# Another rule for the place of split weights, and the state space constants on VectorE alone, woven over a longer stretch

## The chip, the cores and the metric

The kernel runs on one core of a Trainium2 chip. The metric is the device time of one execution in microseconds (us), as the median of several runs. Engines are named as the profile names them: PE is TensorE's matmul, PEld its weight load, DVE is VectorE, ACT is ScalarE, POOL is GpSimd, SP is SyncE, whose queue only issues transfers here.

## What is computed

Two blocks follow each other on 512 tokens (528 with 16 meta tokens in the first) of width 1024. All is float32.

```python
# first block, two layers l = 0, 1
h = h + 0.5 * swiglu(rms_norm(h), ffn1_w_gu[l], ffn1_w_down[l])      # D_FF = 2816
u = rms_norm(h); c_q, c_kv, k_pe, hq, hf, hi, hg, ga, gb = split_cols(u @ w_in[l])
y_a = mla(c_q, c_kv, k_pe, ...) @ w_proj_attn[l]                     # 8 attention heads
y_b = hgrn2(hq, hf, hi, hg, ...) @ w_proj_rec[l]                     # 4 recurrent heads
merged = sigmoid(ga) * y_a + sigmoid(gb) * y_b
h = h + merged @ w_out[l]
h = h + 0.5 * swiglu(rms_norm(h), ffn2_w_gu[l], ffn2_w_down[l])
# second block: an S5 state space branch and a sparse attention branch, merged alike, then a fifth FFN
s = associative_scan(a, b)     # a, b from A_re, A_im, log_dt, B_re, B_im
y = C_re s_r - C_im s_i + D_skip u
```

The state space branch is computed in chunks of eight steps. For that it needs tables worked out from its parameters alone: powers of the complex decay times the input, output and feedback matrices. These are the constants of this case. They depend on nothing that the first block computes.

## The kernel before

Each float32 product is made of three matmuls on rounded operands: high by high, high by low and low by high. A weight is therefore loaded as a raw chunk of 512 KB (tile `raw`, four buffers, issued on SP's queue) and split into a high part `whi` (a copy on ACT) and a low part `wlo` (a subtraction on DVE, in plain stages on POOL for most chunks). Chunks are numbered by first use. There are H = 5 places for split chunks, each a pair of tiles.

**Places.** Chunk i goes into place i % 5, so it may be split only once chunk i - 5 was read for the last time (`allowed`, `hi_lo`). The splits are a queue of steps in order of first use. `between(cost)` is called as PE's work is emitted; it gives credit for steps, up to three at a time, and makes those that are allowed. A step that has not been made by then is made just before the chunk's first use.

**FFN.** There are five. The 22 column blocks j of the hidden layer come as six plain ones and sixteen made of seven products of twelve matmuls each (`product`, 1.46 us of PE in the program's own table of costs). The down projection is done in thirds; for the first two, its steps (`down_steps`, 0.73 us each, of six matmuls) are woven with the products of the next third. A down chunk (consumer operands `gh`, `gl`) is held for seven or eight such steps, with products between, while a chunk for products is read at once. In these stages every engine keeps the order in which the program emits (`self.pin`). The product's results leave the banks through ACT (`tu`, `zu`, `s`) and DVE (`c1`, `c2`, printed `c` in the profile); `gh` and `gl` follow.

**Mixer and merge.** The mixer weaves four pairs of attention and recurrent heads, j = 0 to 3, each with the dense work of the next. With j = 3, the last heads, the gates `ga` and `gb` are woven. Then `merge` follows: an item that frees tiles, eight `project` items (two projections, times gates, sum, split into `mgh` and `mgl`) and seven `w_out` items. Here the tile scheduler decides each engine's order.

**Constants.** `s5_setup_items` gives two lists of items, one for each layer of the first block. They are woven into the merge, from its second item to the fourth from the end. A complex product (`cmul`) is a DVE product `cm`, a POOL product `ct` and their sum, on POOL (tile `cm`) or on DVE (tiles `e`, or `cm` where the sign is turned). `within` makes the feedback matrices `ks` and stores them in 16 small pieces per item, 64 in all, into the DRAM tensor `s5_t` through SP's queue.

Of the kernel before, what the change touches and what calls it, by code (L numbers as in the profile page):

```python
# [281 lines left out]
class Kernel:  # L282
# [46 lines left out]
    def run(self):  # L329
# [6 lines left out]
        raws, sums, made = {}, {}, {}  # L336
        done = [False] * len(order)
        gone = [False] * len(loads)
        n_dma = used = 0
        credit = 0.0  # L340

        def load():
# [7 lines left out]
        def drop(c):  # L350
            raws.pop(c)
            gone[load_at[c]] = True
            while n_dma < len(loads) and (n_dma < self.RAW or gone[n_dma - self.RAW]):
                load()

        def hi_lo(i):
            if i not in made:
                made[i] = [self.wp.tile([128, 1024], F32R, tag=f"{x}{i % self.H}", name=f"w{x}_{i}") for x in ("hi", "lo")]
                n = 1024 if not isinstance(order[i], str) else CHUNKS[order[i]][1] * CHUNKS[order[i]][2]
                nk = 8 if not isinstance(order[i], str) else CHUNKS[order[i]][1]  # L360
                self.split_of[order[i]] = [t[:, :n].rearrange("p (k m) -> p k m", k=nk) for t in made[i]]
            return made[i]
# [62 lines left out]
        def allowed():  # L425
            if n_step == len(queue):
                return False
            i = queue[n_step][0]
            return i < self.H or done[i - self.H]

        def step():
            nonlocal n_step
# [13 lines left out]
                fn()  # L446

        self.between = between
        self.read = lambda c: done.__setitem__(index[c], True)
        load()  # L450
        self.setup(load)
        self.warm()
# [2 lines left out]
        for it in self.prog:  # L455
            if not (it.seven and self.pin):
                for i in range(used):
                    done[i] = True
            self.pin = it.seven
            if not it.seven:  # L460
                between(0.0)
                if it.chunks:
                    while allowed():
                        step()
            used += len(it.chunks)
            while n_step < len(queue) and queue[n_step][0] < used:
                assert allowed()
                step()
            it.fn()
# [540 lines left out]
    def mixer(self, l, st, nxt):  # L1010
# [136 lines left out]
        def hg_dense(j):  # L1147
            items = []
            for n, w in (("f", L), ("i", L), ("q", nq), ("g", nq)):
                items += dense(f"h{n}{l}.{j}", w, times_r(f"z{n}.{j}"))  # L1150
            return items
# [3 lines left out]
        def hg_start(j):  # L1155
            X = XS[j]
            zq, zf, zg = S.pop(f"zq.{j}"), S.pop(f"zf.{j}"), S.pop(f"zg.{j}")
            t = self.alloc("t")
            self.sc.activation(t[:, :L], zf[:, :L], AF.Sigmoid)
            k = self.alloc("k")  # L1160
            self.sc.activation(k[:, :L], zf[:, :L], AF.Sigmoid, scale=-1.0)
            t2 = self.alloc("t2")
            self.sc.activation(t2[:, :nq], zq[:, :nq], AF.Sigmoid)
            t3 = self.alloc("t3")
            self.sc.activation(t3[:, :nq], zg[:, :nq], AF.Sigmoid)
            if l > 0:
                nc.vector.tensor_scalar(t[:, :L], t[:, :L], self.olb[:, j:j + 1], self.lb1[:, j:j + 1], op0=OP.mult, op1=OP.add)
                nc.vector.tensor_scalar(k[:, :L], k[:, :L], self.olb[:, j:j + 1], None, op0=OP.mult)
            nc.vector.tensor_scalar(t[:, :L], t[:, :L], F_MIN, None, op0=OP.max)
            self.sc.preload_act_table_set("natural_log")  # L1170
            self.sc.activation(t[:, :L], t[:, :L], AF.Ln)
            nc.vector.tensor_tensor_scan(zf[:, :L], self.reset[:, :L], t[:, :L], 0.0, op0=OP.mult, op1=OP.add)
            nc.vector.scalar_tensor_tensor(zq[:, :nq], zq[:, :nq], 128 ** -0.5, t2[:, :nq], op0=OP.mult, op1=OP.mult)
            nc.gpsimd.tensor_tensor(zg[:, :nq], zg[:, :nq], t3[:, :nq], op=OP.mult)
            self.free(t, t2, t3)
            X.update(q=zq, b=zf, g=zg, k=k)
# [188 lines left out]
        self.prog += d0[h2:] + [Item(0.5, lambda: hg_start(0))] + qk_items(0)  # L1365
        gates = self.gate_items(str(l), nq, S, st)
        for j in range(4):
            nextd = hg_dense(j + 1) + [Item(0.5, lambda j=j: hg_start(j + 1))] + qk_items(j + 1) if j < 3 else gates
            if j == 2:
                def drop():  # L1370
                    for n in ("cq", "ckv"):
                        hs, ls = S.pop(n)
                        self.free(*hs, *ls)
                    self.free(S.pop("kr"))
                nextd = nextd + [Item(0.0, drop)]
            if j == 3:
                cut = len(gates) - len(gates) // 4
                self.prog += weave(att_items(j) + [Item(0.0, lambda: self.free(*S.pop("v")))], hg_items(j), gates[:cut])
                self.prog += [Item(0.0, lambda: (self.split_y(S, "ya", "ot", nq), self.split_y(S, "yb", "y", nq)))] + gates[cut:]
            else:  # L1380
                self.prog += weave(att_items(j), hg_items(j), nextd)

        at = len(self.prog)
        self.merge(str(l), nq, S, st, nxt)
        if l == 0:
            self.s5_items = self.s5_setup_items()
        m = self.prog[at:]
        self.prog[at:] = m[:1] + weave(m[1:-3], self.s5_items[l]) + m[-3:]


    def reduce_angle(self, t, w):
# [15 lines left out]
    def s5_setup_items(self):  # L1407
# [11 lines left out]
            while stores:  # L1419
                stores.pop(0)()  # L1420

        def store(*pairs, free=()):
            stores.append(lambda: ([nc.sync.dma_start(o, i) for o, i in pairs], self.free(*free)))
        mul, sub, add = OP.mult, OP.subtract, OP.add

        def tt(o, a, b, op, e=None):
            (e or nc.vector).tensor_tensor(o, a, b, op=op)

        def params():
            self.half_pi = self.cst.tile([128, 1], F32, name="half_pi")  # L1430
# [129 lines left out]
        def cmul(qr, s0, y, ri, apart=None):  # L1560

            sl = slice(4 * qr, 4 * qr + 4)

            def v(t):
                if apart is None:
                    return t[:, :512].rearrange("p (i q s) -> p i s q", i=4, s=8)
                return t[:, :512].rearrange("p (i s q) -> p i s q", i=4, s=8)
            pr, pi = (X[k][:, sl, s0:s0 + 8, None].to_broadcast([128, 4, 8, 16]) for k in ("pr", "pi"))  # L1570
            yr, yi = (y[:, 256 * i:256 * i + 256].rearrange("p (i q) -> p i q", q=16)[:, sl, None, :].to_broadcast([128, 4, 8, 16])
                      for i in range(2))
            o, t = self.alloc("cm"), self.alloc("ct")
            tt(v(o), pr, yi if ri else yr, mul)
            tt(v(t), pi, yr if ri else yi, mul, nc.gpsimd)
            if apart is not None:
                for g in range(2):
                    row = slice(64 * g, 64 * g + 64)
                    to = apart[g][32 * ri:32 * ri + 64, :512]
                    nc.vector.scalar_tensor_tensor(to, o[row, :512], -1.0 if ri else 1.0, t[row, :512], op0=mul, op1=sub)  # L1580
            elif ri == 2:
                nc.vector.scalar_tensor_tensor(o[:, :512], o[:, :512], -1.0, t[:, :512], op0=mul, op1=sub)
            else:
                tt(o[:, :512], o[:, :512], t[:, :512], add if ri else sub, nc.gpsimd)
            self.free(t)
            return o

# [21 lines left out]
        def within(qr):  # L1609
            e = X.pop("e")  # L1610
            ks = [self.alloc("ks"), self.alloc("ks")]
            ps = [self.bank(), self.bank()]
            for i in range(4):
                for g in range(2):
                    ti = 4 * qr + i
                    nc.tensor.matmul(ps[g][:16, 128 * i:128 * i + 128], X["cg"][g][:, 16 * ti:16 * ti + 16], e[g][:, 128 * i:128 * i + 128],
                                     start=True, stop=True)
            dd = X["dd"][:16, :32].rearrange("q (i g) -> q i g", g=2)[:, 4 * qr:4 * qr + 4]
            for g in range(2):
                kv = ks[g][:16, :512].rearrange("q (i s p) -> q i s p", i=4, s=8)  # L1620
                nc.vector.tensor_copy(ks[g][:16, :512], ps[g][:16, :512])
                w = self.small.tile([16, 4, 16], F32, name="dsk", bufs=2)
                tt(w, self.ident[:16, None, :16].to_broadcast([16, 4, 16]), dd[:, :, g:g + 1].to_broadcast([16, 4, 16]), mul)
                tt(kv[:, :, 0, :], kv[:, :, 0, :], w, add)
                dst = dr["t"].rearrange("(i g) q j c -> q g i j c", g=2)[:, g, 4 * qr:4 * qr + 4]
                store(*((dst[:, :, j, 16 * j:], ks[g][:16, :512].rearrange("q (i c) -> q i c", i=4)[:, :, :128 - 16 * j])
                        for j in range(8)), free=(ks[g],))
            self.free(*e)

        def in_done():  # L1630
# [468 lines left out]
```

## Time and profile before

| | |
|---|---|
| median of three runs | 3188.55 us (3185.94 to 3188.72) |
| the profiled execution's own time | 3189.57 us |
| its span, first to last instruction | 3187.5 us |
| mean granted clock of TensorE | 0.990 of full speed |
| DVE, ACT and POOL busy | 2182.0, 1436.9 and 785.6 us |

Busy times of engines overlap. The few per cent in which PE was not busy are what an order of work can change, besides the time lost at a lower granted clock. A wait in the profile is idle time before an instruction, put down to the engine and tile that released it last.

### The profile page before, as it was taken

The page shows a single profiled execution, that of the slowest core. Times are in us where ns is not written, and L with a number is a line of the kernel's source. Part 1 is how long each engine was busy: PE and PEld are TensorE (multiplying, and loading weights), DVE is VectorE, ACT ScalarE, POOL GpSimd, SP SyncE. Part 2 cuts the span into 40 slices and gives each one's busy share as a digit, 9 for nine tenths or more (in the row PEclk, how much of TensorE's full clock was granted, in tenths as well). Part 3 has the DMA queues.
Part 4 walks back from the last instruction along what each step waited for, and adds up shares of the span by engine and source line. Part 5 has one row for each costly group of instructions (what it writes and reads, how often), then busy time and mean ns, then how long its engine had stood idle before and what let it go on. Part 6 is the DMA issues. An engine that isn't in the chain of part 4 may idle for free. (4 is left out here: it accounts for less than half of the span.)

```text
span 3187.5 us, 52524 instructions
## 1 busy us (share of the span) xinstructions
PE 3100.3 (97%) x21338; PEld 2849.5 (89%) x21338; DVE 2182.0 (68%) x3752; ACT 1436.9 (45%) x2504; POOL 785.6 (25%) x461
## 2 busy tenths in 40 slices
PE   9999999999999999999999999899999989999999
PEld 9999998999999999999998888688988777788888
DVE  8666666756776666856666764977667587577674
ACT  5444444545444444434444544244446435444442
POOL 2000254444420002100034544530003553320001
PEclk9999999999999999999999999999999999999999
DMA  4232321112322223223321113332334432222332
GB/s 154 91 98 89 112 80 47 41 60 90 123 69 98 91 95 114 80 93 96 104 94 60 47 53 107 104 100 73 105 106 151 125 106 67 67 91 75 99 107 87
DMA packets 107682, 290.90 MB, mean 91 GB/s; under 512 B 23216, under 2 KB 33456, under 8 KB 107440
## 3 DMA queue, kind: packets, MB, share of 16 engines
q1 hardware_dynamic: 107440, 287.55, 28.0%
q8 instruction: 167, 2.74, 0.4%
q14 instruction: 75, 0.61, 0.1%
HBM read 273.61 MB, written 13.89 MB: 90 GB/s over the span
## 5 line engine op out<-in xcount | busy, mean ns | idle before, releaser
L249 POOL TENSOR_TENSOR wlo<-raw,whi 128x1024 fp32r<-128x1024 f32 (+1 forms) x185 | 470.0, 2543 | 2056.9 <-PE bank L249 1101.2
L249 ACT ACTIVATE whi<-raw 128x512 fp32r<-128x512 f32 (+2 forms) x664 | 541.5, 833 | 635.6 <-PE bank L249 301.5
L249 PE MATMUL bank<-xl,whi 128*128 128x264 f32 (+1 forms) x1992 | 664.1, 334 | 4.6 <-DVE xl L249 4.4
L249 PE MATMUL bank<-xh,whi 128*128 128x264 f32 (+1 forms) x1992 | 663.7, 334 | 0.7 <-ACT xh L249 0.7
L249 PE MATMUL bank<-xh,wlo 128*128 128x264 f32 (+1 forms) x1992 | 657.4, 330 | 1.3 <-POOL wlo L249 1.3
L249 DVE TENSOR_TENSOR wlo<-raw,whi 128x1024 fp32r<-128x1024 f32 (+2 forms) x399 | 410.0, 1030 | 156.4 <-ACT whi L249 153.2
L249 PE MATMUL bank<-gh,wlo 128*128 128x264 f32 (+1 forms) x1408 | 441.2, 313 | 15.3 <-DVE wlo L249 15.3
L249 PE MATMUL bank<-gh,whi 128*128 128x264 f32 (+1 forms) x1408 | 440.0, 312 | 0.0
L249 PE MATMUL bank<-gl,whi 128*128 128x264 f32 (+1 forms) x1408 | 439.9, 312 | 0.0
L249 PEld LDWEIGHTS bank<-xl,whi 128*128 128x128 f32 x1992 | 378.5, 190 | 34.1 <-DVE xl L249 6.3
L249 PEld LDWEIGHTS bank<-xh,whi 128*128 128x128 f32 x1992 | 378.1, 190 | 30.0 <-issue 4.1
L249 PEld LDWEIGHTS bank<-xh,wlo 128*128 128x128 f32 x1992 | 378.3, 190 | 27.2 <-issue 1.7
L249 PEld LDWEIGHTS bank<-gh,wlo 128*128 128x128 f32 x1408 | 265.6, 189 | 33.9 <-DVE wlo L249 18.4
L249 PEld LDWEIGHTS bank<-gl,whi 128*128 128x128 f32 x1408 | 265.4, 189 | 8.2
L249 PEld LDWEIGHTS bank<-gh,whi 128*128 128x128 f32 x1408 | 265.6, 189 | 7.8
L249 PE MATMUL bank<-T2h,whi 128*128 128x264 f32 (+1 forms) x640 | 183.8, 287 | 7.7 <-DVE c L249 6.3
L249 PE MATMUL bank<-T2h,wlo 128*128 128x264 f32 (+1 forms) x640 | 182.4, 285 | 2.2 <-DVE wlo L249 2.2
L249 PE MATMUL bank<-B21h,whi 128*128 128x264 f32 (+1 forms) x640 | 181.7, 284 | 1.0 <-ACT zu L249 0.9
L249 PE MATMUL bank<-B21l,whi 128*128 128x264 f32 (+1 forms) x640 | 181.6, 284 | 0.0
L249 PE MATMUL bank<-B21h,wlo 128*128 128x264 f32 (+1 forms) x640 | 181.4, 283 | 0.0
L249 PE MATMUL bank<-T2l,whi 128*128 128x264 f32 (+1 forms) x640 | 181.4, 283 | 0.0
L249 PE MATMUL bank<-T1l,whi 128*128 128x264 f32 (+1 forms) x640 | 181.1, 283 | 0.0
(373 smaller groups left out, 7054.1 us busy)
## 6 DMA issues: line engine op xcount, KB each, us to landing
raw<-in_w_dram SPq DMA_DIRECT2D x423, 512.0 KB, 3.5
raw<-in_w_dram SPq DMA_DIRECT2D x80, 448.0 KB, 3.2
h<-in_x_dram SPq DMA_DIRECT2D x8, 264.0 KB, 6.3
s_win<-cm SPq DMA_DIRECT2D x8, 256.0 KB, 2.9
s_t<-zero SPq DMA_DIRECT2D x8, 256.0 KB, 3.7
s_wo<-cm SPq DMA_DIRECT2D x16, 128.0 KB, 2.6
s<-s_win SPq DMA_DIRECT2D x8, 256.0 KB, 4.0
s<-s_wo SPq DMA_DIRECT2D x8, 256.0 KB, 4.9
```

The lines of the kernel that those rows point to most:

```text
L249: i = f(*args, **kw)
```

## The change

Three things are edited. The place of a split chunk is no longer i % 5: any place that was never used or whose chunk was read can be taken, and of those the one read longest ago is. The constants are woven from the start of the last heads (`at` is now taken at the start of each j, and so holds that of j = 3) up to all but the last two items of the merge. And `cmul` does both of its products and the sum on DVE, while the 64 small stores of `ks` are issued on ACT's queue.

```diff
+        places, read_at = [None] * self.H, list(range(-self.H, 0))
+        clock = 0
...
+        def vacant(k):
+            return places[k] is None or done[places[k]]
+
+        def read(i):
+            nonlocal clock
+            if not done[i]:
+                clock += 1
+                done[i] = True
+                for k in range(self.H):
+                    if places[k] == i:
+                        read_at[k] = clock
...
-                made[i] = [self.wp.tile([128, 1024], F32R, tag=f"{x}{i % self.H}", name=f"w{x}_{i}") for x in ("hi", "lo")]
+                at = min((k for k in range(self.H) if vacant(k)), key=lambda k: read_at[k])
+                places[at], read_at[at] = i, None
+                made[i] = [self.wp.tile([128, 1024], F32R, tag=f"{x}{at}", name=f"w{x}_{i}") for x in ("hi", "lo")]
...
-            i = queue[n_step][0]
-            return i < self.H or done[i - self.H]
+            return queue[n_step][0] in made or any(vacant(k) for k in range(self.H))
...
         for j in range(4):
+            at = len(self.prog)
...
-        at = len(self.prog)
         self.merge(str(l), nq, S, st, nxt)
...
-        self.prog[at:] = m[:1] + weave(m[1:-3], self.s5_items[l]) + m[-3:]
+        self.prog[at:] = weave(m[:-2], self.s5_items[l]) + m[-2:]
...
-            tt(v(t), pi, yr if ri else yi, mul, nc.gpsimd)
+            tt(v(t), pi, yr if ri else yi, mul)
...
-                tt(o[:, :512], o[:, :512], t[:, :512], add if ri else sub, nc.gpsimd)
+                tt(o[:, :512], o[:, :512], t[:, :512], add if ri else sub)
...
-                      for j in range(8)), free=(ks[g],))
+                      for j in range(8)), free=(ks[g],), queue=nc.scalar)
```

How instructions move: 24 `ct` and 12 `cm` instructions go from POOL to DVE, and 64 issues go from SP to ACT. PE has the same matmuls, in nearly the same order.

DVE in the first FFN, where the low part of down chunk 31 is made (`wlo_31`; chunks 30 and 32 are for products). Before:

```order
L249 TENSOR_TENSOR wlo_30_1661<-raw_22_1428,whi_30_1660 128x1024
L249 TENSOR_TENSOR raw_23_1592<-s1_187_1663,raw_22_1428 128x512
L249 TENSOR_TENSOR c2_178_1538<-bank_181_1541,zu_180_1540 128x264
L249 TENSOR_TENSOR c1_177_1537<-bank_186_1635,tu_179_1539 128x264
L249 SCALAR_TENSOR_TENSOR c2_178_1538<-c2_178_1538,s_189_1708 128x264
L249 SCALAR_TENSOR_TENSOR c2_178_1538<-bank_181_1541,s_189_1708 128x264
L249 TENSOR_TENSOR gl_191_1737<-c2_178_1538,gh_190_1736 128x528
L249 TENSOR_TENSOR wlo_31_1745<-raw_24_1649,whi_31_1744 128x1024
```

The same place now:

```order
L249 TENSOR_TENSOR wlo_30_1612<-raw_22_1428,whi_30_1611 128x1024
L249 TENSOR_TENSOR raw_23_1503<-s1_184_1614,raw_22_1428 128x512
L249 TENSOR_TENSOR wlo_31_1664<-raw_24_1600,whi_31_1663 128x1024
L249 TENSOR_TENSOR c2_179_1554<-bank_182_1557,zu_181_1556 128x264
L249 TENSOR_TENSOR s4_189_1714<-raw_23_1503,raw_22_1428 128x512
L249 TENSOR_TENSOR wlo_32_1712<-raw_23_1503,whi_32_1711 128x512
L249 TENSOR_TENSOR c1_178_1553<-bank_188_1650,tu_180_1555 128x264
```

The low part of chunk 31 stood behind the last five evacuations of a block j, and now stands ahead of three that follow.

DVE late in the merge of layer 1, around the sum of the gated projections of block 6 (`ga_6`, `gb_6`) and its split. Before:

```order
L249 TENSOR_TENSOR cm_2501_23176<-pr_2413_22565,s5b_2412_22563 128x4x8x16
L249 TENSOR_TENSOR dsk_23157<-ident_1072,s5d_2417_22573 16x64
L249 TENSOR_TENSOR ga_6_2405_22462<-bank_2471_22953,ga_6_2405_22462 128x512
L249 TENSOR_TENSOR gb_6_2407_22495<-bank_2472_22954,gb_6_2407_22495 128x512
L249 TENSOR_TENSOR ga_6_2405_22462<-ga_6_2405_22462,gb_6_2407_22495 128x512
L249 TENSOR_TENSOR cm_2517_23282<-pr_2413_22565,s5b_2412_22563 128x512
L249 TENSOR_TENSOR mgl_2474_22983<-ga_6_2405_22462,mgh_2473_22982 128x512
L249 TENSOR_TENSOR ga_7_2409_22528<-bank_2481_23023,ga_7_2409_22528 128x512
L249 SCALAR_TENSOR_TENSOR e_2503_23183<-cm_2517_23282,ct_2518_23283 64x512
L249 SCALAR_TENSOR_TENSOR e_2504_23184<-cm_2517_23282,ct_2518_23283 64x512
```

The same place now:

```order
L249 TENSOR_TENSOR ga_6_2440_22596<-bank_2487_23038,ga_6_2440_22596 128x512
L249 TENSOR_TENSOR gb_6_2444_22650<-bank_2488_23039,gb_6_2444_22650 128x512
L249 TENSOR_TENSOR wlo_411_22990<-raw_315_22780,whi_411_22989 128x1024
L249 TENSOR_TENSOR mgl_2486_23027<-ga_5_2411_22453,mgh_2485_23026 128x512
L249 TENSOR_TENSOR ga_6_2440_22596<-ga_6_2440_22596,gb_6_2444_22650 128x512
L249 TENSOR_TENSOR ga_7_2450_22693<-bank_2495_23087,ga_7_2450_22693 128x512
L249 TENSOR_TENSOR mgl_2490_23068<-ga_6_2440_22596,mgh_2489_23067 128x512
L249 TENSOR_TENSOR gb_7_2452_22726<-bank_2496_23088,gb_7_2452_22726 128x512
```

The constants between the merge's own instructions are gone here; they stand earlier, among the last heads and the first projections.

ACT among the last heads of layer 1, around the copy of weight chunk 397 (`p` is a softmax, `X` a decay, `pt` a transposed softmax). Before:

```order
L249 ACTIVATE whi_396_22044<-raw_300_21785 128x1024
L249 ACTIVATE X_2346_22082<-X_2346_22082 128x128x2 x2
L249 ACTIVATE whi_397_22103<-raw_301_21849 128x1024
L249 ACTIVATE p_2351_22118,sm_22120<-p_2351_22118,nm_22119 128x400
L249 ACTIVATE dq_2353_22134<-dk_2352_22133 128x512
```

The same place now:

```order
L249 ACTIVATE whi_396_22094<-raw_300_21812 128x1024
L249 ACTIVATE X_2367_22152<-X_2367_22152 128x128x2 x2
L249 DMA s5_t_74<-ks_2360_22106 16x4x128
L249 DMA s5_t_74<-ks_2360_22106 16x4x112
L249 DMA s5_t_74<-ks_2360_22106 16x4x96
L249 DMA s5_t_74<-ks_2360_22106 16x4x80
L249 ACTIVATE whi_397_22173<-raw_301_21886 128x1024
L249 DMA s5_t_74<-ks_2360_22106 16x4x64
L249 DMA s5_t_74<-ks_2360_22106 16x4x48
L249 DMA s5_t_74<-ks_2360_22106 16x4x32
L249 ACTIVATE p_2372_22188,sm_22190<-p_2372_22188,nm_22189 128x400
```

ACT now issues stores between its instructions, in four clusters of 16, of which this is the first.

## Rows read from the trace of the kernel before

**Rows 1.** The page's first part: busy us, share of the span, instructions.

```profile
PE 3100.3 (97%) x21338; PEld 2849.5 (89%) x21338; DVE 2182.0 (68%) x3752; ACT 1436.9 (45%) x2504; POOL 785.6 (25%) x461
```

**Rows 2.** PE's waits over the whole span: total us, times, longest us.

```profile
PE bank L249 <- DVE wlo L249: 17.5, 20, 1.8
...
PE bank L249 <- DVE c L249: 6.3, 8, 0.9
...
PE bank L249 <- ACT tu L249: 1.4, 3, 1.0
```

**Rows 3.** Timeline of 138 to 146 us: start, duration, engine, [idle before, releaser].

```profile
139.94 1.06 ACT L249 ACTIVATE whi<-raw 128x1024 fp32r<-128x1024 f32 x1 [2.46 <-PE bank L249]
...
141.28 0.28 PE L249 MATMUL bank<-gh,whi 128*128 128x264 f32 x1
...
141.40 0.28 PE L249 MATMUL bank<-gl,whi 128*128 128x264 f32 x1
...
142.19 1.22 DVE L249 TENSOR_TENSOR wlo<-raw,whi 128x1024 fp32r<-128x1024 f32 x1
...
143.47 0.39 PE L249 MATMUL bank<-gh,wlo 128*128 128x264 f32 x1 [1.78 <-DVE wlo L249]
```

**Rows 4.** Timeline of 218 to 228 us, DVE and PE.

```profile
225.62 1.22 DVE L249 TENSOR_TENSOR wlo<-raw,whi 128x1024 fp32r<-128x1024 f32 x1
...
227.84 0.39 PE L249 MATMUL bank<-T2h,whi 128*128 128x264 f32 x1 [0.89 <-DVE c L249]
```

**Rows 5.** Three windows: length, busy us of each engine, granted clock, DMA share, GB/s.

```profile
1008.60:1012.00 3.40, 3.40 (x16) 3.40 (x17) 3.40 (x7) 1.58 (x2) 0.00 (x0) 0.50 0.71 240
800.40:807.20 6.80, 6.04 (x27) 6.07 (x28) 6.80 (x11) 6.70 (x10) 3.16 (x2) 0.50 0.42 161
2056.50:2063.40 6.90, 4.18 (x10) 3.32 (x11) 6.81 (x8) 0.11 (x1) 2.11 (x2) 0.51 0.33 91
```

**Rows 6.** PE's waits in the merge of layer 0, 770 to 890 us.

```profile
PE bank L249 <- DVE ga L249: 5.1, 3, 3.0
PE bank L249 <- DVE gb L249: 1.9, 2, 1.7
```

**Rows 7.** PE's waits in the merge of layer 1, 2000 to 2110 us.

```profile
PE bank L249 <- DVE mgl L249: 3.7, 2, 3.0
PE bank L249 <- ACT mgh L249: 3.7, 1, 3.7
PE bank L249 <- DVE ga L249: 1.8, 1, 1.8
```

**Rows 8.** Windows: heads 0 to 2, last heads, merge; columns as in rows 5.

```profile
450.00:650.00 200.00, 194.96 (x1504) 180.43 (x1504) 138.07 (x344) 102.09 (x236) 96.37 (x79) 0.99 0.15 48
650.00:770.00 120.00, 120.00 (x962) 115.81 (x962) 64.74 (x170) 52.95 (x103) 49.67 (x30) 1.00 0.23 72
780.00:820.00 40.00, 33.01 (x241) 32.02 (x240) 39.15 (x49) 25.33 (x34) 27.87 (x14) 0.91 0.38 124
1690.00:1890.00 200.00, 188.10 (x1199) 166.64 (x1198) 133.31 (x291) 100.21 (x218) 98.73 (x76) 0.96 0.15 47
1890.00:2000.00 110.00, 110.00 (x558) 90.67 (x557) 58.31 (x104) 48.20 (x88) 52.81 (x33) 1.00 0.33 100
```

**Rows 9.** The constants' instructions by tile: ns least/median/most, first and last start.

```profile
L249 DVE TENSOR_TENSOR cm<-pr,s5b x16: 692/1186/2847, 1958.1 to 2061.2; 128x512 f32<-128x512 f32 x16
...
L249 POOL TENSOR_TENSOR cm<-cm,ct x12: 1263/1528/1992, 789.3 to 2053.1; 128x512 f32<-128x512 f32 x12
...
L249 POOL TENSOR_TENSOR ct<-pi,s5b x16: 1054/1501/1809, 1976.5 to 2065.4; 128x512 f32<-128x512 f32 x16
...
L1423 SPq DMA_DIRECT2D s_t<-ks x64: 325/424/1640, 2034.5 to 2096.3; - x64
```

**Rows 10.** Timeline of 794 to 800 us in the merge of layer 0, POOL and DVE.

```profile
795.72 2.83 POOL L249 TENSOR_TENSOR wlo<-raw,whi 128x1024 fp32r<-128x1024 f32 x1
...
796.23 2.89 DVE L249 TENSOR_TENSOR ga<-ga,gb 128x528 f32<-128x528 f32 x1
```

More of the change, by code (lines that the diff above doesn't have):

```diff
@@ L448, in run @@
         self.between = between
-        self.read = lambda c: done.__setitem__(index[c], True)
+        self.read = lambda c: read(index[c])
         load()
@@ L457, in run @@
                 for i in range(used):
-                    done[i] = True
+                    read(i)
             self.pin = it.seven
@@ L1420, in flush, with store, tt @@
                 stores.pop(0)()
-        def store(*pairs, free=()):
-            stores.append(lambda: ([nc.sync.dma_start(o, i) for o, i in pairs], self.free(*free)))
+        def store(*pairs, free=(), queue=nc.sync):
+            stores.append(lambda: ([queue.dma_start(o, i) for o, i in pairs], self.free(*free)))
         mul, sub, add = OP.mult, OP.subtract, OP.add
-        def tt(o, a, b, op, e=None):
-            (e or nc.vector).tensor_tensor(o, a, b, op=op)
+        def tt(o, a, b, op):
+            nc.vector.tensor_tensor(o, a, b, op=op)
         def params():
```

## The prediction

> **What bounds the kernel.** I read the busy shares first. PE is busy for 3100.3 of 3187.5 us [rows 1], so this kernel is PE's matmuls plus about 87 us of holes, plus what PE loses while its clock is lowered. DVE at 2182.0 us and POOL at 785.6 us have room on average. Nothing can be won here but holes and lowered clock; so the next view is the list of PE's waits, over the span and then by stretch.
>
> The largest entry of that list is the low part of a split weight, `wlo`: 17.5 us in 20 waits; `c`, an evacuation of the FFN's products, has 6.3 us in 8 [rows 2]. Taken FFN by FFN, the same list puts practically all of both into the five FFNs, four `wlo` waits in each. A timeline of one shows the mechanism [rows 3]. The copy `whi` of a down chunk starts on ACT at 139.94, after 2.46 us in which ACT waited for PE: its place was still held. From there on the chain is serial. ACT's copy ends at 141.00, DVE's subtraction runs from 142.19 to 143.41 behind another instruction, and PE, which had started `gl,whi` at 141.40, starts `gh,wlo` at 143.47. At this place PE's starts are 0.12 us apart (141.28, 141.40), so 1.95 us are lost where the profile shows an idle time of 1.78: 0.17 more per wait. The `c` waits have the same source. The late `wlo` of 1.22 us at 225.62 stands ahead of an evacuation on DVE, and PE waits 0.89 us for that at 227.84 [rows 4].
>
> The second cluster is the two merges. PE waits 5.1 + 1.9 = 7.0 us in that of layer 0 [rows 6] and 3.7 + 3.7 + 1.8 = 9.2 us in that of layer 1 [rows 7], for DVE's gated sums and their split. There DVE is full, 39.15 of 40 us, while among the last heads just before, it is busy for 64.74 of 120 us and 58.31 of 110, and PE there has no hole at all [rows 8].
>
> The third thing is the clock. Around such waits the granted clock falls to 0.50 of full speed, 1.2 instead of 2.4 GHz: for 3.40 us of PE's work right behind the `wlo` wait of the second FFN, for 6.04 us in the first merge and 4.18 us in the second, where PE had just stood for about 3 us [rows 5 to 7]. Work done at half speed loses half its time: 1.7, 3.0 and 2.1 us.
>
> **The places.** Before, a down chunk held for 7 or 8 woven steps keeps its place, and the chunk five later stands still though other places are vacant. With the new rule the queue of splits stops only when all five places are full. By the order of instructions `wlo_31` now stands ahead of the evacuations that it stood behind, and the low part of such a chunk is made 7 to 12 us of PE's work ahead of its use instead of 0 to 4. As 1.95 us was the longest delay, the waits should go: 17.5 + 6.3 us of idle time and 28 times 0.17 us are 28.6 us. What of it returns? At the ends of the thirds, products stand without down steps between, so PE asks for an evacuation every 1.46 us while the same splits have to be made. By the order I count up to 15 such places, three in each FFN, at which an evacuation may now be late. What such a lateness costs has no row for these places; the nearest is the wait for `tu`, 1.4 us in 3 [rows 2], or 0.47 us, and the mean of the `c` waits, 6.3 us in 8 or 0.79, is the upper end. I take 15 times 0.47 = 7.0 us; the bounds are 0 and 15 times 0.79 = 11.8. So the FFNs give 21.6 us (16.8 to 28.6), and the clock behind the `wlo` wait 1.7 more. Splitting as such costs nothing new: the same copies and subtractions run on the same engines.
>
> **The constants.** Three things happen to them. They start some 100 us earlier, from the beginning of the last heads. Their 24 `ct` and 12 `cm` go from POOL to DVE. And 64 stores go from SP to ACT.
>
> DVE gains 36 instructions. Their nearest rows are its own products `cm` of the same tile, 0.69 us at the least and 1.19 in the median [rows 9]: 36 of them are 24.8 to 42.8 us over both layers. Layer 1 has 20 of the 36, 13.8 to 23.8 us, and 16 `cm` that were already there, 19.0 us at the median; that is up to 42.8 us, and the last heads of layer 1 leave DVE 110 - 58.31 = 51.7 us free [rows 8]. In layer 0 the last heads leave 55.3 us. The cover of this term is therefore DVE's free time among the last heads, and if that cover failed the 24.8 to 42.8 us would come on top of merges that are already full. POOL loses 24 products and 12 sums at a median of 1.50 and 1.53 us [rows 9], about 54 us, which nothing waits for by itself.
>
> By the order, the late part of the merge of layer 1 loses its constants between `ga`, `gb` and `mgl`, but four or five groups of them remain among the first projections, as they do in smaller number in layer 0. I take all the waits of [rows 6, 7] as gone: 7.0 + 9.2 us, 9 waits at 0.17 us more, 1.5 us, and 3.0 + 2.1 us of clock, together 22.8 us. Its bounds are in the next term, as what remains and what comes new are not told apart by any row.
>
> Given back: the last heads become like the heads before them, where DVE is busy for 138.07 of 200 us and 133.31 of 200, and PE has holes of 200 - 194.96 = 5.0 us in layer 0 and 200 - 188.10 = 11.9 us in layer 1 [rows 8]. At those rates 120 us of last heads cost 3.0 us, and 110 us cost 6.5, together 9.5, where there is nothing now. Not all of those holes are DVE's, so this is no low value. The lower bound is nothing. The upper one adds that half of the merges' idle time, 8.1 us, and both lowered clocks, 5.1 us, stay: 22.7 us. I take 9.5.
>
> The stores: an issue took 0.42 us in the median on SP [rows 9], and 64 are 27 us. On ACT they lie between the copies of weights, which by the order are made 9 us of PE's work or more ahead of use, and ACT is busy for 48.20 of 110 us there [rows 8]. A cluster of 16 issues takes 6.8 us. That is within the 9, and it is split by other instructions. I cost it at nothing; if a `p` or a gate stood behind a cluster and PE waited, each cluster could cost up to 6.8 us. SP's queue loses the 27 us, and raw chunks behind it come sooner, for which nobody waits.
>
> **The sum.** 21.6 + 1.7 + 22.8 - 9.5 = 36.6 us less than the profiled 3189.57 us: 3153.0. The median of the runs is 1.0 us lower than the profiled execution, so 3152 us is forecast. With every wait gone and nothing returned it is 28.6 + 1.7 + 22.8 = 53.1 us less, or 3135.5 us. With the smaller FFN term and the full return it is 16.8 + 1.7 + 22.8 - 22.7 = 18.6 less, or 3170 us.
>
> **Where POOL and DVE meet.** POOL's `wlo` at 795.72 took 2.83 us, and a DVE sum that started within it, 0.51 us later, took 2.89 [rows 10]; the constants' own `cm` range from 0.69 to 2.85 us [rows 9]. POOL keeps splitting two of three weight chunks in these stages. By the Trainium skill (SBUF — State Buffer, section "SBUF: two separate sides") VectorE and GpSimd share a pair of ports that is locked for a whole instruction, and the other engine is blocked until it ends; this trace agrees, with the 2.89 us. By that rule the moved instructions trade POOL's interference with each other's for a stop of up to one split's length each time that one starts beside a split, and the removed POOL products no longer stop DVE.
>
> **Rivals.**
> - *The merges' gain only moves.* The waits reappear among the last heads, where PE now has none, since heads wait for DVE too: the holes of heads 0 to 2 speak for it [rows 8]. The free 51.7 and 55.3 us of DVE speak against. Then only the FFN's 21.6 + 1.7 us are left: 3165 us.
> - *DVE stops beside POOL's splits.* Every moved instruction takes 1.19 us instead of 0.69, 18 us more, and PE feels all of it: 3170 us. For it speaks [rows 10]; against it, that the merges now lose the 54 us of POOL's constants, which stopped DVE as well.
> - *Nothing changes.* If the freed splits merely push other instructions on ACT and DVE back, PE waits for evacuations as long as it did for `wlo`: 3189 us. The waits for a place [rows 3] speak against it, since idle time of ACT was in them.
> - *Slower: bursts of splits ahead of evacuations.* Once any vacant place will do, up to three split steps can be made at once in front of an evacuation, in every one of the 80 blocks j made of products (16 in each of 5 FFNs), not at the ends of thirds alone. Its price is that of [rows 4], 0.89 us behind one `wlo`. At 0.89 us in each, 71 us: 3223 us. It decides from 36.6 / 80 = 0.46 us per block. Against it: among woven steps, by the order, evacuations keep at least 1.4 us of PE's work before their use.
> - *All is gained*, 3135 us, with no late evacuation and no new hole.
>
> **Chances.** Both gains, with the returns about as worked out: 0.62. Only the FFN's: 0.16. Stops beside POOL: 0.07. No change: 0.06. Slower by bursts: 0.05. All gained: 0.04. The likeliest case's own time is 3152 us. The range, 3135 to 3171 us, takes in the bounds of the unknown returns and the first two rivals, and leaves out 0.11 and the tails of these. Runs of this kernel differ by 2.8 us, so some 0.2%, 6.4 us, is what can be told from no change: faster 0.89, same 0.06, slower 0.05.
>
> **What the profile of the changed kernel would show.** If the places work, PE's list has no wait for `wlo` in the FFNs, and ACT's copy of a down chunk no longer follows a wait for PE. Waits for `tu`, `zu` or `c` of 0.3 to 0.8 us at the ends of thirds would confirm the return, and such waits in every block the bursts. If the constants work, DVE in 780 to 820 us is well under 39 of 40 us, POOL has about 54 us less in all, no window of the merges shows a clock of 0.50, and the last heads show at most some 10 us of new holes; DVE's `ct` near 0.69 us would say that POOL does not stop it. A wait of PE for `p`, `kt` or a gate right behind ACT's stores would make the term of the stores wrong. What would make the forecast wrong as a whole is a clock that falls in new places, since one hole of a few us brings several us of half speed with it.

## The result and the profile after

The changed kernel takes 3143.64 us, the median of four runs (3142.73 to 3144.44), against 3187.36 us before: a ratio of 0.9857 (95% interval 0.9843 to 0.9871). That is 43.7 us less; 36.6 were forecast from the profiled execution, and the time lies inside the range.

The page's first part after, answering to [rows 1]:

```profile
PE 3083.0 (98%) x21338; PEld 2840.3 (90%) x21338; DVE 2195.7 (70%) x3788; ACT 1442.3 (46%) x2502; POOL 735.9 (23%) x425
```

The span is 3141.2 us, so PE's holes have shrunk from 87 to 58 us. PE is also busy for 17 us less with the same matmuls: less lowered clock (the mean granted clock is 0.994, it was 0.990), and a matmul that had to wait counts as busy for a little longer (0.39 us in [rows 3], where its neighbours have 0.28). PE's waits over the span after, answering to [rows 2]:

```profile
PE bank L249 <- ACT kt L249: 14.5, 6, 4.1
...
PE bank L249 <- ACT ktm L249: 4.1, 4, 1.3
...
PE bank L249 <- ACT tu L249: 3.3, 8, 0.9
...
PE bank L249 <- ACT zu L249: 0.4, 2, 0.2
```

VectorE's `wlo`, `c`, `ga`, `gb` and `mgl`, and ACT's `mgh`, are no longer in the list at all. What is new is small in the FFNs (`tu`, `zu`) and larger among the heads (`kt` was 8.3 us in 4 waits before). The place in the first FFN that [rows 3] show, in the timeline after:

```profile
128.93 1.06 ACT L249 ACTIVATE whi<-raw 128x1024 fp32r<-128x1024 f32 x1 [1.74 <-PE bank L249]
...
130.03 1.22 DVE L249 TENSOR_TENSOR wlo<-raw,whi 128x1024 fp32r<-128x1024 f32 x1 [0.91 <-ACT whi L249]
...
131.99 0.43 DVE L249 TENSOR_TENSOR c<-bank,zu 128x264 f32<-128x264 f32 x1 [0.74 <-PE bank L249]
...
139.26 0.28 PE L249 MATMUL bank<-gh,wlo 128*128 128x264 f32 x1
```

The low part of the down chunk is ready at 131.25 and is used at 139.26: 8.0 us ahead. ACT still waits for PE before the copy, but where nobody waits for ACT. Windows of the last heads (first and third row) and the merges, answering to [rows 8]; columns as in [rows 5]:

```profile
640.00:770.00 130.00, 126.65 (x1013) 121.86 (x1012) 100.27 (x214) 72.80 (x136) 55.14 (x32) 1.00 0.28 90
780.00:820.00 40.00, 40.00 (x333) 40.00 (x332) 29.96 (x44) 12.70 (x16) 11.98 (x5) 1.00 0.32 101
...
1850.00:1980.00 130.00, 124.55 (x630) 101.45 (x629) 98.28 (x158) 50.06 (x94) 60.36 (x31) 0.99 0.33 97
1980.00:2020.00 40.00, 40.00 (x180) 31.93 (x180) 36.50 (x49) 12.04 (x17) 8.10 (x4) 1.00 0.35 101
2020.00:2060.00 40.00, 40.00 (x180) 31.79 (x179) 26.72 (x29) 13.84 (x19) 13.00 (x5) 1.00 0.37 113
```

The merges have no hole left, and DVE there went from 39 of 40 us to 27 to 37. The last heads, without a hole before, have 3.4 and 5.5 us of them.

To place the microseconds, the start of each matmul was compared with that of the same matmul in the trace of before. The table gives what each stage gained or lost against before, in us of one profiled execution each, for the changed kernel and the experiments below:

| kernel | five FFNs | last heads 0 | merge 0 | last heads 1 | merge 1 | rest | span |
|---|---|---|---|---|---|---|---|
| changed | -31.3 | 5.6 | -12.9 | 11.3 | -16.2 | -2.8 | -46.3 |
| e1 places only | -31.4 | 0.0 | 0.0 | 0.1 | 0.1 | -3.5 | -34.7 |
| e2 constants only | 1.7 | 5.6 | -12.9 | 12.7 | -16.1 | -3.4 | -12.4 |
| e3 range only | 0.7 | 5.5 | -12.8 | 14.2 | -16.4 | 3.1 | -5.7 |
| e4 engine only | -0.1 | 0.0 | 2.1 | 0.0 | 0.0 | 2.8 | 4.8 |
| e5 old gate | -18.2 | 5.6 | -12.8 | 11.3 | -16.1 | 1.4 | -28.8 |
| e6 newest place | -23.1 | 5.7 | -12.9 | 11.6 | -15.9 | -0.9 | -35.5 |
| e7 stores on SP | -31.3 | 5.7 | -12.9 | 11.3 | -16.5 | -1.0 | -44.7 |
| e8 products on POOL | -31.3 | 5.6 | -12.9 | 14.1 | -16.5 | 1.6 | -39.4 |
| e9 from a quarter | -32.0 | 8.9 | -12.2 | 3.3 | -8.8 | -2.9 | -43.7 |
| e10 from the middle | -31.2 | 1.1 | -6.2 | 2.1 | -6.6 | -1.6 | -42.4 |
| e11 four places | -19.4 | 5.4 | -12.8 | 15.1 | -15.9 | -6.0 | -33.6 |
| e12 before, four places | 251.6 | 0.2 | 0.2 | -0.1 | 2.9 | -12.6 | 242.2 |

The column "rest" has all other stages. Part of it is lowered clock that falls elsewhere from execution to execution (before has 3.4 us of it about 19 us into the span, the changed kernel none there, and that is 1.6 of its 2.8 us); the rest of it was not taken apart. The executions profiled for e3 and e11 were the slowest of theirs, 3183.69 and 3155.74 us against medians of 3178.54 and 3148.94. Of the losses in the last heads, 3.7 us in layer 1 are matmuls of the constants that moved there from the merge (two of the four groups that multiply `e` and `cg`, 16 matmuls of 0.116 us each), and some 1.8 us in layer 0 the transposes of `cm` (four of eight groups of four, 0.45 us each).

### The profile page after: what moved, and what is told of

It is laid out like the page before. It is cut to its first block, busy times and chain, and to the rows that moved or that the text cites. A ratio compares the mean times of both kernels' runs of the same rounds, so it can differ in the third digit from the quotient of the medians.

```text
span 3141.2 us, 52812 instructions
## 1 busy us (share of the span) xinstructions
PE 3083.0 (98%) x21338; PEld 2840.3 (90%) x21338; DVE 2195.7 (70%) x3788; ACT 1442.3 (46%) x2502; POOL 735.9 (23%) x425
## 3 DMA queue, kind: packets, MB, share of 16 engines
q1 hardware_dynamic: 102320, 286.37, 28.6%
## 5 line engine op out<-in xcount | busy, mean ns | idle before, releaser
L249 DVE TENSOR_TENSOR wlo<-s,whi 128x512 fp32r<-128x512 f32 x240 | 159.6, 686 | 43.5 <-ACT whi L249 39.6
```

Of the source, the lines that this page charges most:

```text
L249: i = f(*args, **kw)
```

## The experiments

**The two edits apart.** e1 is before with the new rule for places alone; e2 is before with the three edits of the constants alone.

> Only the rule for the places is changed; the constants are as before. First theory: the five FFNs give about 31 us on their own, as the stages of the changed kernel's trace are shorter by 6.9, 8.4, 5.8, 4.9 and 5.5 us, so about 3156 us, and the merges stand as before. Rival: part of that came from the constants' instructions being elsewhere, and the forecast's 23 us is all that the places give: about 3164 us.

> The constants are changed in full (range, engine, stores), the places are as before. First theory: the two edits are independent, so about 12 us are gained, 23 in the merges and 10 to 11 given back among the last heads: about 3175 us. Rival: with places held, splits in the last heads or the merge come late too, and the gain is under 5 us: 3183 us or more.

Measured: e1 3155.09 us, ratio 0.9889 (0.9876 to 0.9903); e2 3178.18 us, ratio 0.9963 (0.9950 to 0.9975). The first theory holds for both: each edit changes its own stages, and by nearly the same amounts as in the changed kernel (the largest difference is 1.4 us, in the last heads of layer 1). e1 keeps the waits of the merges and has none for `wlo` or `c`:

```profile
PE bank L249 <- DVE ga L249: 7.0, 4, 3.0
...
PE bank L249 <- ACT tu L249: 3.3, 8, 0.9
...
PE bank L249 <- DVE mgl L249: 3.0, 1, 3.0
PE bank L249 <- ACT mgh L249: 2.3, 1, 2.3
```

**Range and engine apart.** e3 and e4 are before with one of these lines each:

```diff
-        self.prog[at:] = m[:1] + weave(m[1:-3], self.s5_items[l]) + m[-3:]
+        self.prog[at:] = weave(m[:-2], self.s5_items[l]) + m[-2:]      # e3, with at taken at the start of j = 3
...
-            tt(v(t), pi, yr if ri else yi, mul, nc.gpsimd)
+            tt(v(t), pi, yr if ri else yi, mul)                        # e4, and the sum alike
```

> Before with only the longer range of weaving; products and sums stay on POOL, stores on SP. First theory: the gain comes from spreading DVE's constants, so most of the 12 us is here: 3175 to 3179 us. Rival: POOL's products stopping DVE are the cause, so waits only move to the last heads: 3185 us or more.

> Before with only the products and sums moved from POOL to DVE; range and stores as before. First theory: DVE is full in the merges, so 36 more instructions at 0.69 to 1.19 us make them longer, by up to 15 us: 3187 to 3202 us. Rival: without POOL's products DVE's own instructions run at 0.69 us and the merges get shorter: 3178 us.

Measured: e3 3178.54 us, ratio 0.9967 (0.9955 to 0.9980); e4 3191.00 us, ratio 1.0004 (0.9995 to 1.0013). The range alone does what all three edits do, and the engine alone does nothing that can be told. With the products on DVE inside the full merge, PE's waits in layer 1 add up to what they were, 9.1 us against 9.2, but one of them, for ACT's `mgh`, is now 7.5 us long; in layer 0 the merge is 2.1 us longer. From 1990 to 2110 us of e4:

```profile
PE bank L249 <- ACT mgh L249: 8.9, 2, 7.5
PE bank L249 <- DVE mgl L249: 0.2, 1, 0.2
```

**Gate and choice apart.** The new rule does two things: a split may be made earlier, and its place is the one read longest ago. e5 undoes the first, e6 turns the second round, both in the changed kernel.

```diff
-            return queue[n_step][0] in made or any(vacant(k) for k in range(self.H))
+            i = queue[n_step][0]                                       # e5
+            return i < self.H or done[i - self.H]
...
-                at = min((k for k in range(self.H) if vacant(k)), key=lambda k: read_at[k])
+                at = max((k for k in range(self.H) if vacant(k)), key=lambda k: read_at[k])   # e6
```

> The changed kernel, in which a chunk still goes to the place that has been free for longest, but may be split only once the chunk five before it was read, as before. First theory: the FFNs gain by being allowed to split earlier, so the waits for the low part come back and most of 31 us with them: about 3172 us. Rival: the choice of the place is what counts, since a copy into a place read long ago waits for nothing: 3143 to 3150 us.

> The changed kernel with one word turned round: of the vacant places the one that was read last is taken. In the FFNs the engines' order is the same, so only what a copy waits for differs. First theory: being allowed early is all; seldom is more than one place vacant, and the loss is under 6 us: 3143 to 3149 us. Rival: copies wait on ACT for PE's last read, evacuations behind them come late, and at least half of the FFNs' 31 us is lost: 3159 us or more.

Measured: e5 3159.67 us, ratio 0.9901 (0.9887 to 0.9916); e6 3153.56 us, ratio 0.9884 (0.9867 to 0.9900). Neither theory holds alone: both expected one part to be nearly all. With the old gate 18.2 of 31.3 us remain from the choice of the place; with the new gate and the choice turned round 23.1 remain. What is lost in e5 is the waits of before, shorter; PE's waits over its span:

```profile
PE bank L249 <- DVE wlo L249: 5.5, 13, 0.7
...
PE bank L249 <- DVE c L249: 4.0, 8, 0.7
```

In e6 no wait of PE for VectorE's `wlo` is left, but evacuations come late:

```profile
PE bank L249 <- ACT zu L249: 4.2, 7, 0.9
...
PE bank L249 <- ACT tu L249: 3.8, 11, 0.6
...
PE bank L249 <- DVE c L249: 1.4, 1, 1.4
```

The order of instructions is that of the changed kernel but for 60 of 2430 on ACT and 95 of 3788 on DVE, so what differs is what copies wait for. How it gets from there to PE is shown in part only: the longest `zu` wait, at 2881 us, has ACT's `zu` behind a copy that idled 2.35 us for DVE's `raw`, where the same copy idles 1.44 us in the changed kernel; which wait for a place made DVE late was not followed.

**How scarce the places are.** e11 is the changed kernel and e12 the kernel before, both with `H = 4`.

> The changed kernel with four places in place of five. First theory: places are what the FFNs' splits wait for, and a held down chunk leaves three of four; a part of the 31 us is lost, so 3150 to 3170 us, still under 3189. Rival: with a free choice five places are more than are needed, and four cost nothing: 3147 us or less.

> The kernel before with four places, so that chunk i waits for chunk i - 4. First theory: the wait for one held place is the cause of the FFNs' waits, so a shorter cycle makes them longer, by at least the 31 us that they are now: 3220 us or more. Rival: the waits come from when the steps are made and not from places: within 10 us of before, under 3199 us.

Measured: e11 3148.94 us, ratio 0.9871 (0.9855 to 0.9888); e12 3437.01 us, ratio 1.0775 (1.0755 to 1.0795). With the fixed rule one place less costs 246 us, and PE's waits are those of [rows 2], grown eightfold:

```profile
PE bank L249 <- DVE wlo L249: 148.1, 101, 3.3
PE bank L249 <- ACT whi L249: 25.5, 30, 1.1
```

So the fixed cycle of places is what the FFNs waited for. With the free rule four places are still better than five with the fixed one. The loss against the changed kernel is about 5 us by the medians; of e11's expectations the time lies a little under the first theory's span, and the rival's "cost nothing" is not refuted by the interval. In the profiled execution, 7.5 of the 11.9 us by which its FFNs lie behind the changed kernel's are one place in the first FFN: PE waits 5.8 us for `tu` at 92.6 us, with 6.8 us of lowered clock behind it.

**Stores and products taken back.** In the changed kernel, e7 issues the stores on SP again and e8 does the products and sums on POOL again.

```diff
-                      for j in range(8)), free=(ks[g],), queue=nc.scalar)
+                      for j in range(8)), free=(ks[g],))               # e7
...
-            tt(v(t), pi, yr if ri else yi, mul)
+            tt(v(t), pi, yr if ri else yi, mul, nc.gpsimd)             # e8, and the sum alike
```

> The changed kernel with the 64 small stores issued on SP's queue again. First theory: they are covered on either queue, so within 3 us of the changed kernel: 3141 to 3147 us. Rival: clusters of 16 issues on ACT delay what the last heads wait for (about 7 us of stops in layer 1), and that returns: 3137 us or less.

> The changed kernel with the second product and the sum of the constants on POOL again. First theory: the range carries the gain and the engine carries little, so 3141 to 3149 us. Rival: POOL's products beside DVE's stop DVE again among the last heads, and 6 us or more are lost: 3150 us or more.

Measured: e7 3144.50 us, ratio 0.9855 (0.9840 to 0.9869); e8 3149.06 us (3141.91 to 3150.41), ratio 0.9865 (0.9850 to 0.9881). The stores are free on either queue, as costed. e8 lies at the upper edge of the first theory with overlapping intervals, so it is not settled by time. Of the stages that the edits touch, its trace differs in one place: the wait for `kt` in the last heads of layer 1 is 5.4 us instead of 4.1, with 6.8 instead of 3.4 us at the lowered clock, 2.8 us by the table. e3, which also has the products on POOL, has the same 5.4 us there.

**Where the return comes from.** The changed kernel, 1868 to 1877 us, in the last heads of layer 1:

```profile
1868.37 2.78 POOL L249 TENSOR_TENSOR wlo<-raw,whi 128x1024 fp32r<-128x1024 f32 x1
...
1869.41 2.81 DVE L249 TENSOR_TENSOR cm<-pr,s5b 128x512 f32<-128x512 f32 x1
...
1872.25 0.69 DVE L249 SCALAR_TENSOR_TENSOR cm<-cm,ct 128x512 f32<-128x512 f32 x1
...
1873.06 0.68 DVE L249 TENSOR_TENSOR cm<-pr,s5b 128x512 f32<-128x512 f32 x1
1873.65 0.68 DVE L249 CUSTOM_DVE_ANT_0 p<-bank,mask 128x512 f32<-128x512 f32 x1
...
1875.13 0.73 ACT L249 ACTIVATE p<-p,nm 128x528 f32<-128x528 f32 x1 [4.40 <-DVE nm L249]
...
1875.87 0.47 ACT L249 ACTIVATE kt<-bank 128x384 f32<-128x384 f32 x1
...
1876.39 0.28 PE L249 MATMUL bank<-ident,kh 128*16 128x128 f32 x1 [4.09 <-ACT kt L249]
```

Read from the end: PE waits 4.09 us for `kt`, which on ACT stands behind a softmax `p`, which waits 4.40 us for DVE's maximum, which stands behind three constants, the first of which took 2.81 us beside POOL's split of 2.78 (a product like it took 1.10 to 1.24 us where POOL was idle). With the lowered clock behind it this one place costs 5.8 us. e9 and e10 start the constants later, past that head:

```diff
+        at += (len(self.prog) - at) // 4        # e9; // 2 in e10; just ahead of self.merge
         self.merge(str(l), nq, S, st, nxt)
```

> The changed kernel with the constants woven from after the first quarter of the last heads' items instead of from their start. First theory: the stops early in the last heads (the waits for kt, 7.6 us in layer 1 with the lowered clock behind them, 2.9 in layer 0) come from constants on VectorE ahead of a head's softmax; they go, the merges stay without waits, and 6 to 10 us are gained on the changed kernel: about 3135 us. Rival: a stop among the last heads comes wherever constants and heads meet, so it only moves: 3141 to 3147 us.

> As the quarter, but from the middle of the last heads' items. First theory: the early stops go as well, and VectorE has still room in the second half (about 65 us of heads and 80 us of merge in layer 1), so 3134 to 3138 us. Rival: the denser constants bring waits for the gated sums back into the merges, up to the 23 us of before: 3145 to 3160 us.

Measured: e9 3146.75 us, ratio 0.9871 (0.9854 to 0.9887); e10 3147.54 us, ratio 0.9866 (0.9852 to 0.9881). The added waits for `kt` are gone in both (8.2 us in 4 over the span, 8.3 in 4 before), so the constants caused them. But nothing is won: e9 has waits at other places in the last heads of layer 0 and both have waits in the merges again, here those of e10 from 640 to 860 and from 1845 to 2080 us:

```profile
PE bank L249 <- DVE ga L249: 2.3, 1, 2.3
PE bank L249 <- DVE gb L249: 0.8, 1, 0.8
...
PE bank L249 <- ACT mgh L249: 2.9, 1, 2.9
PE bank L249 <- DVE e L249: 0.9, 1, 0.9
```

By the table, heads and merge together give -7.3, -3.3 and -5.1 us in layer 0 and -4.9, -5.5 and -4.5 in layer 1, for the three starts. The rivals describe this better than the first theories. No version that clearly beats the changed kernel was found.

## Why the prediction was right, point by point

- *What bounds the kernel* was right: all that was won is holes of PE and lowered clock.
- *The places*: the direction and the stages were right, a size was off. The term gave 21.6 us and 1.7 of clock; the stages measured 31.3, and e1 35 us in time (31 to 40). The mis-sized step is what the delays were worth: 28.6 us were taken, and matmul by matmul (the same comparison as for the table) they were about 37. The 28 waits for `wlo` and `c` all went, with 23.9 us of idle time, but they had cost 32.9, the 1.5 us of clock behind one of them apart: 0.32 us more for each and not 0.17. The matmul behind the one that waited starts late as well: after the wait of 143.47 in [rows 3] the next start is 0.22 us on, where other starts are 0.12 apart, so that wait cost 2.05 us.

```profile
143.69 0.28 PE L249 MATMUL bank<-gh,whi 128*128 128x264 f32 x1
```

Twelve smaller delays that the list of waits does not show gave 2.9 us more, and two waits for `zu` 1.0. The return was near: 5.8 us at 14 places where 7.0 at up to 15 were taken, though the list shows only seven of them, with 2.4 us of idle time. Shifts too small to tell apart take back another 1 us. One of the new waits, in the first FFN:

```profile
227.25 0.39 PE L249 MATMUL bank<-T2h,whi 128*128 128x264 f32 x1 [0.35 <-ACT tu L249]
227.48 0.28 PE L249 MATMUL bank<-T2l,whi 128*128 128x264 f32 x1
```

- *The mechanism of the places* was told too simply. The forecast put it down to being allowed earlier. e5 and e6 show that it is as much the place: of 31.3 us, 13.1 go with the gate alone, and 8.2 when the choice is turned round. One sign was wrong as well: ACT's wait for PE ahead of a copy does not vanish. Over the span it grew, and at the place shown above it costs nothing, because the copy is early. ACT's copies of raw chunks before and after, with the idle time ahead of them and its releasers:

```profile
L249 ACT ACTIVATE whi<-raw 128x512 fp32r<-128x512 f32 (+2 forms) x664 | 541.5, 833 | 635.6 <-PE bank L249 301.5 <-issue 240.5 <-DVE raw L249 44.5
```

```profile
L249 ACT ACTIVATE whi<-raw 128x512 fp32r<-128x512 f32 (+2 forms) x664 | 544.6, 835 | 776.8 <-PE bank L249 452.2 <-issue 241.6 <-DVE raw L249 28.9
```

- *The merges*: forecast 22.8 us. Measured 12.9 + 16.2 = 29.1, of which 1.8 + 3.7 are matmuls that merely moved: 23.6. All waits of [rows 6, 7] and both lowered clocks are gone.
- *Given back*: forecast 9.5 us. Measured 5.6 + 11.3 = 16.9, less the same 5.5: 11.4. The size came from a likeness to heads 0 to 2, and that it is near is in part luck: those wait for `kt` without any constants (8.3 us in 4), while e9 and e10 show that here constants on DVE caused the waits, 5.8 us of them at one place.
- *The engine move and the stores* were costed at nothing, and nothing can be told from noise: e4 and e7. DVE's instructions for constants took 93.5 us instead of 58.2, so 35.3 more, within the 24.8 to 42.8 that were taken; its busy time grew by 13.7 only, as other work on it took less, and which was not followed. POOL lost 49.7 us, where about 54 were forecast. That the merges' relief would come in part from POOL's removed products was not needed: e3 has it all with POOL's products in place.
- *The rivals*: that the merges' gain only moves was half true (11.4 of 23.6). That DVE stops beside POOL's splits is shown at the place that cost 5.8 us with the clock, where it made one constant some 1.6 us longer; that is included in the return, and it did not decide the time. Late evacuations, which the rival of the bursts asked for, are seen in e6, at 8.2 us for 80 blocks, 0.10 us each where 0.46 would have decided.
- The rest, 2.8 us, has 1.6 us of lowered clock that fell elsewhere in this execution; what made the other 1.2 is open. Of the 9.7 us between the forecast 36.6 and the 46.3 of the two profiled executions, the FFNs have 8.0, the merges 0.8 and the rest 2.8, less 1.9 that the heads gave back beyond the forecast.

## What to carry to other kernels

A buffer that is assigned by counting makes everything wait for the one user that holds it longest; a free choice of the buffer read longest ago costs nothing at run time, and here made four buffers better than five. Test how scarce a resource is by taking one away: 246 us against about 5 said more than any list of waits. Work off the critical path that is spread over a longer stretch pays where the stretch's own waits are fewer; how the two balance is worked out from the waits in both, and once the engine is even, shifting the start only moves them.

## What was not expected of the hardware

The 1.19 us of `cm`, which the forecast read as an instruction slowed by POOL, are mostly the instruction itself. The constants' tiles after, on DVE alone; ns least/median/most:

```profile
L249 DVE TENSOR_TENSOR cm<-cm,ct x12: 678/694/2634, 710.5 to 1972.9; 128x512 f32<-128x512 f32 x12
L249 DVE TENSOR_TENSOR cm<-pr,cb x8: 1096/1162/1233, 707.2 to 767.6; 128x512 f32<-128x512 f32 x8
...
L249 DVE TENSOR_TENSOR ct<-pi,s5b x16: 672/1120/2540, 1851.9 to 2009.0; 128x512 f32<-128x512 f32 x16
```

The products with `cb` stay between 1.10 and 1.23 us in all eight cases, and the plain sums of the same 128x512 take 0.69 in the median. The order in which the result is written goes with the two values. `cmul` writes a product through one of two views, and reads operands of the same shape for both (`apart` is given for the products of the tiles `e`):

```python
            def v(t):
                if apart is None:
                    return t[:, :512].rearrange("p (i q s) -> p i s q", i=4, s=8)
                return t[:, :512].rearrange("p (i s q) -> p i s q", i=4, s=8)
```

The first view writes neighbours eight elements apart, the second one after the other. In the trace after, 29 of the 32 products of the first kind take 1.10 to 1.24 us, and 13 of the 16 of the second kind 0.67 to 0.69.

The rest are stops beside POOL, and they follow a simple sum. In the trace of before, 26 of DVE's 44 instructions for constants started while POOL was idle, and none took longer than 1.19 us. The other 18 started inside an instruction of POOL, and each took longer: to the end of POOL's, and in 10 of the 12 that write in order 0.55 us more. After, 15 of 80 are stopped, such as this sum, which lasts 2.05 us to the end of POOL's split and then 0.55 (five more started inside an instruction of POOL and were not stopped; why is open):

```profile
709.90 2.67 POOL L249 TENSOR_TENSOR wlo<-raw,whi 128x1024 fp32r<-128x1024 f32 x1 [5.95 <-ACT whi L249]
...
710.52 2.60 DVE L249 TENSOR_TENSOR cm<-cm,ct 128x512 f32<-128x512 f32 x1
```
